# Grouped-query attention on one core: new constants in an instruction planner, one more chain of approximate exponentials, and a bank for the first keys

## The chip, the core and the metric

The kernel runs on one core of a Trainium2 chip. TensorE multiplies matrices into PSUM, ScalarE (ACT) evaluates exponentials, VectorE (DVE) does elementwise work, GpSimd (POOL) and the DMA queues move and cast data. The metric is device time in microseconds (us). The kernel before takes 366.95 us, the median of three runs from 366.82 to 367.03; the profiled execution has a span of 365.6 us.

## What is computed

Batch 8, 8 query heads and 2 key/value heads, sequence 1024, head size 64, all float32 in and out. Four query heads share one key/value head.

```python
scores = scale * np.matmul(q_group, k_group.transpose(0, 1, 3, 2))   # scale = 1/sqrt(64)
attn = np.exp(scores - scores_max)
attn = attn / (np.sum(attn, axis=-1, keepdims=True) + 1e-08)
output = np.matmul(attn, v_group)
```

So there are 64 jobs (8 x 8 heads), each with a 1024 x 1024 matrix of scores, which must be exponentiated, multiplied with the values and divided by its row sums. The inputs are small (0.1 times normal), and the kernel leaves out the subtraction of the maximum.

## The kernel before

**Tiles.** A job's scores come in eight units, one per pair of key blocks. A unit is two matmuls (L537) of 64 x 512, one on each half of the rows of the array, into one of three PSUM slots of 128 x 1024 float32 (sp0, sp1, sp2, two banks each). The scores are transposed: keys lie on partitions, queries along the free dimension. The PV matmuls (L601) take blocks of 128 queries of the exponentials as weights and the values with a column of ones as the moving operand (65 columns), so the row sums come out as column 64. Results gather in two more PSUM banks (op0, op1), seven pieces of 128 queries in a bank. VectorE takes the reciprocal of the sums (L654) and multiplies (L657), and a DMA stores each head.

**Two ways to exponentiate.** Six of a head's eight units go to ScalarE: one activation with Exp (L549), PSUM in, bfloat16 out (tile pt). The other two go to VectorE, which approximates. Its first pass (L560, "dpass") reads the slot and writes 16-bit integers that are the bits of an approximate power of two (tile yt). Then, for two units together (a "chain"), L567 ("zh") and L574 ("two") split mantissa and exponent with bit operations into zt and et, and L583 ("mul") multiplies. The term et is not added by VectorE but by TensorE: a unit of VectorE costs two PV terms per piece instead of one. Only in the last two heads does VectorE add it (L588).

**The order.** The class Plan runs before any instruction is written. It simulates the engines with the constants M_..., in ns, and lists events in the order in which they are to be issued; the kernel then writes them in that order, under a manual schedule. So each engine's queue has a fixed order, and all true times come from semaphores. Some constants are prices (M_ACT an exp, M_ATAIL its tail, M_FIX the fixed part of a VectorE operation, M_DTAIL its tail, M_REC a reciprocal); others are policy. M_RUNWAY says how much work ScalarE may have ahead when a further unit of scores is issued for it, M_BACK how much VectorE may have, M_WAIT how long TensorE holds out for a slot before it turns to PV, M_START and M_SWAP when the slots, ScalarE and VectorE begin, M_WARM until when scores cost double, M_Q1 when the second head's queries are there. MXD is how many of a head's units VectorE may take: `pick_d` chooses the head. When TensorE has nothing else to do early on, it runs dummy matmuls (L429).

**Self-waits.** pt has 32 buffers. When a buffer comes round again it must not be written before its last write is known to be done. Every twelfth exp is given a wait for the exp fifteen before it, so that the framework has that knowledge at hand.

**The start.** The first head's q and k come straight to SBUF, are cast to bfloat16, and turned by TensorE with an identity (L443): four blocks of q into sp1, four of k into sp2. ScalarE copies 384 columns of q out (L453), VectorE the first 128 of k (L454), the rest of q (L455), the rest of k (L456). Then the first scores run, and `swap_k0` builds the copy of k with its halves exchanged (L462, L466).

**Other work.** GpSimd issues DMAs that cast later heads' q and k to bfloat16 in DRAM (L359, L367), and copies the values into the tile va, as bfloat16 with the ones between them (L384), once for each of the 16 key/value heads.

Of the kernel before, what the change touches and what calls it, by code (L numbers as in the profile page):

```python
# [8 lines left out]


M_START = 5850
M_SWAP = 1100
M_Q1 = 3300
M_QSTEP = 2700
M_WARM = 5900
M_FILL = 12000
M_DUMMY = 110
M_SEE = 51
# [2 lines left out]
M_SWITCH = 93  # L21
M_MM = 31.2
M_PVTAIL = 180
M_ACT = 905
M_ATAIL = 135
M_FIX = 76
M_DTAIL = 83
M_DEP = 34
M_D1 = 1.042
M_D2 = 0.521  # L30
M_D4 = 0.261
M_REC = 115
M_GAP = 90
M_RUNWAY = 1500
M_BACK = 3000
M_WAIT = 250
STEP = 10
INF = float("inf")
PB = 7
NPIECE = 8  # L40
GRAIN = 1
MXD = 2
TAIL = 2
STEPS = (("zh", M_D4), ("two", M_D4), ("mul", M_D2), ("add", M_D2))


class Plan:
# [14 lines left out]
    def run(self):  # L62
        nj, ev = self.nj, self.ev
        todo = [list(range(8)) for _ in range(nj)]
        dcount = [0] * nj
        qready = [M_START] + [M_START + M_Q1 + M_QSTEP * j for j in range(nj - 1)]
        slot_free = [M_START, M_START, M_START + M_SWAP - 600]
        aq, dq = [], []
        p_ready = [[INF] * 8 for _ in range(nj)]
        tP = tA = M_START  # L70
        tD = M_START + M_SWAP
        mode = None
# [3 lines left out]
        norms = []  # L76
        out_free = [M_START, M_START]
        pc, done = 0, 0
# [6 lines left out]
        def steps_of(j):  # L85
            return STEPS if j >= nj - TAIL else STEPS[:3]

        def pick_d():
            for j in range(a, min(nj, a + 3)):
                if todo[j] and dcount[j] < MXD and qready[j] <= tP:  # L90
                    return j
            return None

        while pc < last or steps or norms:
# [3 lines left out]
            if tA == t:  # L98
                if aq and aq[0][0] <= t:
                    _, s, j, c = aq.pop(0)  # L100
                    ev.append((t, "act", s, j, c))
                    tA = t + M_ACT
                    slot_free[s] = p_ready[j][c] = tA + M_ATAIL + M_SEE
                else:
                    tA = t + STEP
                continue
            if tD == t:
                end = None
                if dq and dq[0][0] <= t:
                    _, s, j, c = dq.pop(0)  # L110
# [11 lines left out]
                    ev.append((t, "dpass", s, (ch["id"], len(ch["pairs"]) - 1), (j, c)))  # L122
                    end = t + M_FIX + 1024 * M_D1
                    slot_free[s] = end + M_DTAIL + M_SEE
                    dlast = (ch["id"], 0)
# [3 lines left out]
                elif norms and norms[0][0] <= t and norms[0][1] == "rec":  # L129
                    _, _, lo, hi = norms[0]  # L130
                    ev.append((t, "rec", (lo, hi), None, None))
                    end = t + M_REC
                    dlast = lo
                    norms[0] = (end, "norm", lo, hi)
                else:
# [10 lines left out]
                    if best:  # L146
                        at = max(t, dend + M_DEP) if best[0] else t
                        ch = best[2]
                        if ch is None:
                            _, _, lo, hi = norms.pop(0)  # L150
                            ev.append((t, "norm", (lo, hi), None, None))

                            end = at + M_FIX + 64 * min(hi - lo, PB if lo < last else 4) * M_D1
                            out_free[group_of[lo] % 2] = end + M_DTAIL + M_SEE
                            dlast = None
                        else:
                            n = len(ch["pairs"])
                            kind, rate = ch["steps"][ch["at"]]
                            ev.append((t, kind, None, ch["id"], n))
                            end = at + M_FIX + 1024 * n * rate  # L160
                            ch["at"] += 1
                            dlast = (ch["id"], ch["at"])
                            if ch["at"] == len(ch["steps"]):
                                chains.remove(ch)
                                for j, c in ch["pairs"]:
                                    p_ready[j][c] = end + M_DTAIL + M_SEE
                if end:
                    tD, dend = end, end + M_DTAIL
                else:
                    tD = t + STEP  # L170
                continue

            cold = 2 if t < M_WARM else 1
            free = [s for s in range(3) if slot_free[s] <= t]
            runway = tA - t + M_ACT * len(aq)
            slack = runway - cold * M_PAIR - M_PTAIL - (M_SWITCH if mode != "s" else 0)
            can_a = a < nj and len(aq) < 2 and qready[a] <= t and used_p < self.npt
            dj = None
            if not dq and len(chains) < self.nyt and (open_chain or used_c < self.nct):
                back = max(tD - t, 0)  # L180
                for ch in chains:
                    n = len(ch["pairs"])
                    back += sum(M_FIX + 1024 * n * r for _, r in ch["steps"][ch["at"] :])
                if back < M_BACK:
                    dj = pick_d()
            kind = None
            if free:
# [5 lines left out]
                elif can_a:  # L193
                    full = len(free) > 1 or mode == "s"
                    if slack <= M_GAP or (full and runway < M_RUNWAY):
                        kind = "A"
            if kind:
# [4 lines left out]
                j = a if kind == "A" else dj  # L202
                c = todo[j].pop(0)
# [7 lines left out]
                else:  # L211
                    dcount[j] += 1
                    if j < nj - TAIL:
                        self.mms[j] += 1
            elif (
                mode == "s"
                and (dj is not None or (can_a and runway < M_RUNWAY + M_WAIT))
                and any(t < x <= t + M_WAIT for x in slot_free)
            ):
                tP += STEP  # L220
            elif pc < last and (
# [12 lines left out]
                if done == total:  # L234
# [6 lines left out]
                    if pc % NPIECE == 0:  # L241
                        j = pc // NPIECE - 1
# [6 lines left out]
            elif (  # L249
# [12 lines left out]
                c = min(steps, key=lambda c: p_ready[nj - 1][c])  # L262
# [13 lines left out]
            if open_chain and not dq and a >= nj - 2 and pick_d() is None:  # L276
                chains.append(open_chain)
                open_chain = None
# [5 lines left out]
def kernel(  # L284
# [7 lines left out]
    nc = tc.nc  # L292
# [5 lines left out]
    Sync = mybir.DependencyInfo(mybir.DependencyClass.Sync, mybir.DependencyReason.DATA)  # L298
# [14 lines left out]
    NPT = 32  # L313
# [24 lines left out]
    def new_slot(i):  # L338
        sps[i] = banks[f"sp{i}"].tile([128, 2, HS], FP32, name=f"sp{i}")
        return sps[i]  # L340
# [33 lines left out]
    def rows(x, fours=False):  # L374
        how = "(p c two) d -> p c (two d)" if fours else "(c p two) d -> p c (two d)"
        return x.rearrange(how, p=128, two=2)

    def load_v(b, g):
        t = vsp.tile([128, NH, 2 * D], FP32, name="vs")
        vs[(b, g)] = t  # L380
        return nc.sync.dma_start(out=t, in_=rows(v[b, g], b == g == 0))
# [34 lines left out]
    k0, q0 = kt[(0, 0)], qt[0]  # L416
# [20 lines left out]
    nc.scalar.activation(out=b16["k"][:, 1:NH], in_=f32["k"][:, 1:NH], func=AF.Copy)  # L437

    tc.add_manual_dep(load_v(0, 0).ins, ins.ins.name, Sync, reason="loads in time, not sooner")
    turned = {"k": new_slot(2)[:, 0, :], "q": new_slot(1)[:, 0, :]}  # L440

    def turn(x, c):
        nc.tensor.matmul(  # L443
            turned[x][:, c * 128 : (c + 1) * 128],
            lhsT=b16[x][:, c, :], rhs=ident, start=True, stop=True,
        )

    for c in range(NH):
        turn("q", c)
    for c in range(NH):  # L450
        turn("k", c)
    QS = 3 * 128
    nc.scalar.activation(out=q0[:, 0, 0:QS], in_=turned["q"][:, 0:QS], func=AF.Copy)  # L453
    nc.vector.tensor_copy(out=k0[:, 0, 0:128], in_=turned["k"][:, 0:128])  # L454
    nc.vector.tensor_copy(out=q0[:, 0, QS:HS], in_=turned["q"][:, QS:HS])  # L455
    nc.vector.tensor_copy(out=k0[:, 0, 128:HS], in_=turned["k"][:, 128:HS])  # L456

# [13 lines left out]
    for j in range(NJ):  # L471
# [8 lines left out]
        if h % HPG == 0:  # L480
            ev.append((max(pvs[j] - 8000, M_START), "pl", None, (b, g), None))
        if j > 2:
# [17 lines left out]
    exps, stores = [], []  # L500

    def terms(j, par):

        for ci in range(NC):
            c = ci if par == 0 else (ci + NH) % NC
            if (j, c) in where:
                ch, i = where[(j, c)]
                if j < NJ - TAIL:
                    yield ci, et[ch].bitcast(BF16)[:, i, par, :]
# [4 lines left out]
    for when, kind, x, j, c in ev:  # L514
# [31 lines left out]
        elif kind == "act":  # L546
# [1 line left out]
            pt[(j, c)] = p  # L548
            exps.append(nc.scalar.activation(out=p, in_=where_s[(j, c)], func=AF.Exp, scale=scale))  # L549

            if len(exps) % 12 == 0 and len(exps) > 16:
                tc.add_manual_dep(
                    exps[-1].ins, exps[-16].ins.name, Sync, reason="buffers written before"
                )
        elif kind == "dpass":
            ch, i = j
            where[c] = j
            if i == 0:
                yt[ch] = yp.tile([128, 2, 2, HS], U16, name="yt")
            nc.vector.tensor_scalar(  # L560
                out=yt[ch][:, i, :, :], in0=where_s[c],
                scalar1=EXP_A, scalar2=EXP_B, op0=ALU.mult, op1=ALU.add,
            )
        elif kind == "zh":
# [3 lines left out]
                out=zt[j][:, 0:c], in0=yt[j][:, 0:c], scalar1=0x7F, scalar2=0x3F00,  # L568
                op0=ALU.bitwise_and, op1=ALU.bitwise_or,
            )  # L570
        elif kind == "two":
# [3 lines left out]
                out=et[j][:, 0:c], in0=yt[j][:, 0:c], scalar1=0x7F80, scalar2=None,  # L575
# [5 lines left out]
        elif kind == "mul":  # L581
            z = zt[j].bitcast(BF16)[:, 0:c]
            nc.vector.tensor_tensor(  # L583
                out=z, in0=yt[j].bitcast(BF16)[:, 0:c], in1=z, op=ALU.mult
            )
        elif kind == "add":
            z = zt[j].bitcast(BF16)[:, 0:c]
            nc.vector.tensor_tensor(  # L588
                out=z, in0=et[j].bitcast(BF16)[:, 0:c], in1=z, op=ALU.add
# [40 lines left out]
        elif kind == "half":  # L630
# [3 lines left out]
                out=rows(out[b, h])[:, 2 * x : 2 * x + 2],  # L634
                in_=ost[:, r : r + 4, :].rearrange("p (s two) d -> p s (two d)", two=2),
            )
        elif kind in ("rec", "norm"):
# [17 lines left out]
            else:  # L655
                n = min(n, PB if lo < plan.last else 4)
                nc.vector.tensor_tensor(  # L657
                    out=ost[:, r : r + n, :],
# [4 lines left out]
                if lo >= plan.last:  # L663
                    for i in range(4):
                        nc.scalar.activation(  # L665
                            out=ost[:, r + 4 + i, :], in_=o2[:, 1, i, 0:D],
                            func=AF.Copy, scale=rec[:, 4 + i : 5 + i],
                        )
        elif kind == "store":
# [3 lines left out]
                out=rows(out[b, h], j == 0),  # L673
                in_=ost[:, r : r + NPIECE, :].rearrange("p (s two) d -> p s (two d)", two=2),
# [32 lines left out]
```

## Time and profile before

| engine | busy us, share of the span | what it does |
|---|---|---|
| ScalarE | 356.4, 97% | 384 exps on line L549, 352.8 us |
| VectorE | 353.4, 97% | 128 first passes 156.0, 64 products 81.6, 72 normalizations 44.3, L567 44.2, L574 42.6, reciprocals 14.2 |
| TensorE, matmul | 345.7, 95% | 1024 score matmuls 172.0 and 5024 PV matmuls |
| TensorE, weight load | 219.5, 60% | |
| GpSimd | 49.8, 14% | 78 DMA issues 38.2, 16 copies of values 11.2 |

TensorE's clock was granted in full (0.999). The DMA engines moved 44.81 MB, 123 GB/s on average. In the list of waits, TensorE's scores waited 6.5 us in all for ScalarE to release a slot (28 times, 0.4 us at most) and 3.6 us for VectorE (12 times); ScalarE's exps waited 1.6 us for scores, VectorE's first passes 0.8.

How to read it: busy time is the union of the spans of an engine's instructions. One exp's span is 1.135 us on average, while 384 of them fit into 352.8 us: a span includes the tail [...], and the next instruction starts within it. A wait that is shorter than the tail does not show as idle time. The spacing from start to start, in the timeline, is what an instruction takes from its engine.

The last exp starts at 358.9 us, the last PV matmuls run from 360.11 to 361.03, and the last normalization on VectorE starts at 361.31; after it come the last stores.

### The profile page before, as it was taken

The page shows a single profiled execution, that of the slowest core. Times are in us where ns is not written, and L with a number is a line of the kernel's source. Part 1 is how long each engine was busy: PE and PEld are TensorE (multiplying, and loading weights), DVE is VectorE, ACT ScalarE, POOL GpSimd, SP SyncE. Part 2 cuts the span into 40 slices and gives each one's busy share as a digit, 9 for nine tenths or more (in the row PEclk, how much of TensorE's full clock was granted, in tenths as well). Part 3 has the DMA queues.
Part 4 walks back from the last instruction along what each step waited for, and adds up shares of the span by engine and source line. Part 5 has one row for each costly group of instructions (what it writes and reads, how often), then busy time and mean ns, then how long its engine had stood idle before and what let it go on. Part 6 is the DMA issues. An engine that isn't in the chain of part 4 may idle for free. (4 is left out here: it accounts for less than half of the span.)

```text
span 365.6 us, 13820 instructions
## 1 busy us (share of the span) xinstructions
PE 345.7 (95%) x6161; PEld 219.5 (60%) x6161; DVE 353.4 (97%) x476; ACT 356.4 (97%) x392; POOL 49.8 (14%) x100
## 2 busy tenths in 40 slices
PE   7899999999999999999999999999999999999994
PEld 3465665666656666566566565666656666556663
DVE  3999999999999999999999999999999999999995
ACT  5999999999999999999999999999999999999995
POOL 4002031121201112021111112012021011111000
PEclk9999999999999999999999999999999999999999
DMA  7446585566664975678764868667496667577213
GB/s 172 88 88 128 111 168 97 134 149 124 121 120 105 148 148 112 148 114 128 131 112 104 168 102 152 127 137 119 85 158 122 158 102 147 118 130 107 74 34 113
DMA packets 89307, 44.81 MB, mean 123 GB/s; under 512 B 45504, under 2 KB 87616, under 8 KB 88000
## 3 DMA queue, kind: packets, MB, share of 16 engines
q1 hardware_dynamic: 86336, 33.31, 40.5%
q0 software_dynamic: 2496, 10.23, 21.9%
q8 instruction: 48, 0.79, 0.9%
q10 hardware_dynamic: 416, 0.39, 0.3%
q14 instruction: 11, 0.09, 0.1%
HBM read 25.17 MB, written 27.00 MB: 143 GB/s over the span
## 5 line engine op out<-in xcount | busy, mean ns | idle before, releaser
L549 ACT ACTIVATE pt<-sp 128x1024 bf16<-128x1024 f32 x384 | 352.8, 1135 | 1.6 <-PE sp L537 1.6
L601 PE MATMUL ops<-va,pt 128*128 128x65 bf16 x3024 | 186.1, 194 | 0.0
L537 PE MATMUL sp<-qt,kt 64*128 64x512 bf16 x1024 | 172.0, 382 | 13.9 <-ACT pt L549 6.5
L601 PEld LDWEIGHTS <-pt 128*128 128x128 bf16 x3024 | 134.9, 97 | 48.3 <-issue 48.3
L560 DVE TENSOR_SCALAR yt<-sp 128x1024 uint16<-128x1024 f32 x128 | 156.0, 1219 | 1.8 <-PE sp L537 0.8
L601 PE MATMUL ops<-va,zt 128*128 128x65 bf16 x1008 | 120.6, 194 | 0.0
L601 PE MATMUL ops<-va,et 128*128 128x65 bf16 x992 | 118.8, 194 | 0.0
L601 PEld LDWEIGHTS <-et 128*128 128x128 bf16 x992 | 80.1, 98 | 17.6 <-issue 16.2
L601 PEld LDWEIGHTS <-zt 128*128 128x128 bf16 x1008 | 81.4, 97 | 14.5 <-issue 14.2
L583 DVE TENSOR_TENSOR zt<-yt,zt 128x2048 bf16<-128x2048 bf16 x64 | 81.6, 1275 | 0.0
L537 PEld LDWEIGHTS <-kt 64*128 64x128 bf16 x1024 | 46.1, 93 | 55.3 <-issue 34.0
L359 POOL DMA_DIRECT2D qd<-in_q_dram x63 | 30.8, 489 | 228.4 <-PE sp L537 223.0
L657 DVE TENSOR_TENSOR ost<-ops,rec 128x448 f32<-128x448 f32 x72 | 44.3, 615 | 0.0
L567 DVE TENSOR_SCALAR zt<-yt 128x2048 uint16<-128x2048 uint16 x64 | 44.2, 691 | 0.0
L574 DVE TENSOR_SCALAR et<-yt 128x2048 uint16<-128x2048 uint16 x64 | 42.6, 666 | 0.0
L367 POOL DMA_DIRECT2D kd<-in_k_dram x15 | 7.4, 493 | 55.2 <-PE sp L537 50.4
L654 DVE RECIPROCAL rec<-ops 128x7 f32<-128x7 f32 x72 | 14.2, 198 | 0.5 <-PE ops L601 0.2
L384 POOL CAST va<-vs 128x512 bf16<-128x512 f32 x16 | 11.2, 700 | 1.2 <-DMA vs<-in_v_dram 1.1
L429 PE MATMUL ops<-warm 128*128 128x128 bf16 (+1 forms) x33 | 5.5, 320 | 1.2 <-DVE warm L351 1.2
L429 PEld LDWEIGHTS <-warm 128*128 128x128 bf16 x33 | 2.4, 108 | 4.1 <-issue 2.9
L434 DVE CAST k<-k 128x128 bf16<-128x128 f32 x1 | 0.2, 226 | 2.5 <-DMA k<-in_k_dram 2.5
L665 ACT ACTIVATE ost<-sp,rec 128x64 f32<-128x64 f32 x4 | 0.9, 315 | 1.8 <-PE sp L622 1.8
(30 smaller groups left out, 16.5 us busy)
## 6 DMA issues: line engine op xcount, KB each, us to landing
out_dram<-ost SPq DMA_DIRECT2D x63, 256.0 KB, 2.9
qd<-in_q_dram POOLq DMA_DIRECT2D x63, 128.0 KB, 3.5
vs<-in_v_dram SPq DMA_DIRECT2D x16, 256.0 KB, 4.0
kd<-in_k_dram POOLq DMA_DIRECT2D x15, 128.0 KB, 3.5
kt<-kt SPq DMA_DIRECT2D x30, 64.0 KB, 3.5
qt<-qd SPq DMA_TRANSPOSE x63, 4.0
q<-in_q_dram ACTq DMA_DIRECT2D x1, 256.0 KB, 3.3
kt<-kd SPq DMA_TRANSPOSE x15, 3.4
```

What stands on the lines that cost most here:

```text
L359: return nc.gpsimd.dma_start(out=t.rearrange("(a x) d -> a (x d)", x=4), in_=q[b, h].rearrange("(a x) d -> a (x d)", x=8),)
L384: return nc.gpsimd.tensor_copy(out=va[:, b * G + g, :, :, 0:D], in_=vs.pop((b, g)).rearrange("p c (two d) -> p c two d", two=2),)
L429: nc.tensor.matmul(ops[1][:, 0:cols], lhsT=warm[:, 0:128], rhs=warm[:, 0:cols], start=True, stop=True)
L537: now = nc.tensor.matmul(sps[x][:, half, :], lhsT=t[lo : lo + D, c // NH, ci % NH * 128 : (ci % NH + 1) * 128], rhs=qt[j][lo : lo + D, 0, ...
L549: exps.append(nc.scalar.activation(out=p, in_=where_s[(j, c)], func=AF.Exp, scale=scale))
L560: nc.vector.tensor_scalar(out=yt[ch][:, i, :, :], in0=where_s[c], scalar1=EXP_A, scalar2=EXP_B, op0=ALU.mult, op1=ALU.add,)
L567: nc.vector.tensor_scalar(out=zt[j][:, 0:c], in0=yt[j][:, 0:c], scalar1=0x7F, scalar2=0x3F00, op0=ALU.bitwise_and, op1=ALU.bitwise_or,)
L574: ins = nc.vector.tensor_scalar(out=et[j][:, 0:c], in0=yt[j][:, 0:c], scalar1=0x7F80, scalar2=None, op0=ALU.bitwise_and,)
L583: nc.vector.tensor_tensor(out=z, in0=yt[j].bitcast(BF16)[:, 0:c], in1=z, op=ALU.mult)
L601: nc.tensor.matmul(ops[plan.group_of[x] % 2][:, lo : lo + D + 1], lhsT=p[:, qs * 128 : (qs + 1) * 128], rhs=va[:, b * G + h // HPG, ci % N ...
L654: nc.vector.reciprocal(out=to, in_=sums)
L657: nc.vector.tensor_tensor(out=ost[:, r : r + n, :], in0=o[:, :, 0:D], in1=rec[:, 0:n].unsqueeze(2).to_broadcast([128, n, D]), op=ALU.mult,)
```

## The change

It has four parts.

1. **Constants of the plan.** The prices of an exp, of VectorE's fixed part and of the tails are set anew, and so are the policy constants. This is meant to bring the plan closer to the measured times, so that the order that it finds fits the chip.
2. **A third unit for VectorE in two heads.** `pick_d` allows three instead of two in heads whose number is 1 modulo 32 (heads 1 and 33). Two units make one chain. They leave ScalarE.
3. **Rarer self-waits.** Every 26th exp waits for the one five before it, instead of every twelfth for the one fifteen before it.
4. **The start.** The first block of k is turned into sp0, a bank of its own, and ScalarE takes 320 instead of 384 columns of the first q.

```diff
-M_START = 5850
-M_SWAP = 1100
-M_Q1 = 3300
+M_START = 5800
+M_SWAP = 1500
+M_Q1 = 3400
-M_WARM = 5900
+M_WARM = 6400
-M_ACT = 905
-M_ATAIL = 135
-M_FIX = 76
-M_DTAIL = 83
+M_ACT = 917
+M_ATAIL = 107
+M_FIX = 66
+M_DTAIL = 80
-M_REC = 115
+M_REC = 90 
-M_RUNWAY = 1500
-M_BACK = 3000
-M_WAIT = 250
+M_RUNWAY = 2200
+M_BACK = 2500
+M_WAIT = 300
...
+MORE = 32
...
-                if todo[j] and dcount[j] < MXD and qready[j] <= tP:
+                if todo[j] and dcount[j] < MXD + (j % MORE == 1) and qready[j] <= tP:
...
-    turned = {"k": new_slot(2)[:, 0, :], "q": new_slot(1)[:, 0, :]}
+    turned = {"k": new_slot(2)[:, 0, :], "q": new_slot(1)[:, 0, :], "k0": new_slot(0)[:, 0, :]}
...
-            turned[x][:, c * 128 : (c + 1) * 128],
+            turned["k0" if x == "k" and c == 0 else x][:, c * 128 : (c + 1) * 128],
...
-    QS = 3 * 128
+    QS = 320
...
-    nc.vector.tensor_copy(out=k0[:, 0, 0:128], in_=turned["k"][:, 0:128])
+    nc.vector.tensor_copy(out=k0[:, 0, 0:128], in_=turned["k0"][:, 0:128])
...
-            if len(exps) % 12 == 0 and len(exps) > 16:
+            if len(exps) % (NPT - 6) == 0:
                 tc.add_manual_dep(
-                    exps[-1].ins, exps[-16].ins.name, Sync, reason="buffers written before"
+                    exps[-1].ins, exps[-6].ins.name, Sync, reason="buffers written before"
                 )
```

## The prediction

> **What bounds the kernel now.** I read the page first, for the load of each engine:
>
> ```profile
> PE 345.7 (95%) x6161; PEld 219.5 (60%) x6161; DVE 353.4 (97%) x476; ACT 356.4 (97%) x392; POOL 49.8 (14%) x100
> L549 ACT ACTIVATE pt<-sp 128x1024 bf16<-128x1024 f32 x384 | 352.8, 1135 | 1.6 <-PE sp L537 1.6
> L560 DVE TENSOR_SCALAR yt<-sp 128x1024 uint16<-128x1024 f32 x128 | 156.0, 1219 | 1.8 <-PE sp L537 0.8
> L583 DVE TENSOR_TENSOR zt<-yt,zt 128x2048 bf16<-128x2048 bf16 x64 | 81.6, 1275 | 0.0
> ```
>
> Three engines are full, so the question is which one really has room. [...] So I went to the timeline of ScalarE, where exps that follow each other without a visible gap are merged:
>
> ```profile
> 6.84 27.74 ACT L549 ACTIVATE pt<-sp 128x1024 bf16<-128x1024 f32 x30 [1.11 <-PE sp L537]
> ...
> 109.93 5.74 ACT L549 ACTIVATE pt<-sp 128x1024 bf16<-128x1024 f32 x6
> 115.84 2.91 ACT L549 ACTIVATE pt<-sp 128x1024 bf16<-128x1024 f32 x3 [0.16 <-PE sp L537]
> ```
>
> Thirty exps in 27.74 us are (27.74 - 1.14)/29 = 0.917 us apart; from the first start (6.84) to the last (358.9, the answer on line L549) the mean is 352.05/383 = 0.919. The closest spacing in the trace is 0.904 (thirteen in a row from 66.88 to 78.63 us). So ScalarE needs 383 x 0.904 = 346.2 us and loses about 5.8 in waits too short to be listed as idle.
>
> The same for VectorE. Its timeline gives the spacing of each operation, start to start:
>
> ```profile
> 111.50 2.01 DVE L583 TENSOR_TENSOR zt<-yt,zt 128x2048 bf16<-128x2048 bf16 x1
> 113.43 1.21 DVE L560 TENSOR_SCALAR yt<-sp 128x1024 uint16<-128x1024 f32 x1
> ...
> 115.24 1.21 DVE L560 TENSOR_SCALAR yt<-sp 128x1024 uint16<-128x1024 f32 x1
> 116.37 0.61 DVE L657 TENSOR_TENSOR ost<-ops,rec 128x448 f32<-128x448 f32 x1
> 116.90 0.68 DVE L574 TENSOR_SCALAR et<-yt 128x2048 uint16<-128x2048 uint16 x1
> 117.50 0.19 DVE L654 RECIPROCAL rec<-ops 128x7 f32<-128x7 f32 x1
> 117.62 1.17 DVE L583 TENSOR_TENSOR zt<-yt,zt 128x2048 bf16<-128x2048 bf16 x1
> 118.71 1.21 DVE L560 TENSOR_SCALAR yt<-sp 128x1024 uint16<-128x1024 f32 x1
> 119.84 0.61 DVE L657 TENSOR_TENSOR ost<-ops,rec 128x448 f32<-128x448 f32 x1
> 120.37 0.68 DVE L567 TENSOR_SCALAR zt<-yt 128x2048 uint16<-128x2048 uint16 x1
> 120.97 1.21 DVE L560 TENSOR_SCALAR yt<-sp 128x1024 uint16<-128x1024 f32 x1
> ```
>
> A first pass (L560) takes 1.13, L567 and L574 take 0.60 each, a product (L583) 1.09 to 1.13, a normalization (L657) 0.53 and its reciprocal (L654) 0.115. With the counts of the page: 128 x 1.13 + 64 x (0.60 + 0.60 + 1.11) + 2 x 1.09 (L588) + 73 x 0.645 = 342 us of pure work. VectorE runs from 7.80 (first pass) to 361.31 (last normalization), 353.5 us. The missing 11.5 us have two parts. The product of 111.50 took 2.01 instead of 1.2, because GpSimd was copying values at that moment:
>
> ```profile
> 111.80 0.63 POOL L384 CAST va<-vs 128x512 bf16<-128x512 f32 x1
> ```
>
> That slot came free late, and the exp of 115.84 above started 0.46 us late. Products average 1.275 against 1.17 to 1.22 undisturbed, so about 64 x 0.075 = 4.8 us, and L567 (0.691 against 0.64 to 0.69) adds some 0.7: **5.5 us of collisions**. The other **6 us are waits**: 0.57 between the first two passes, 0.75 before the last reciprocals, and some 4.7 spread over the middle. TensorE waited 6.5 us for ScalarE's slots and 3.6 for VectorE's, so it is close behind. No engine has 2% to give; VectorE has 6 us of waits, ScalarE 5.8.
>
> [...] the first key copy (L454), which needs one key block, starts at 5.67, after the fourth block was turned (5.63), [...] the trace shows 0.904, which I use.
>
> **The change part by part.** From the instruction lists of both programs as built: 382 exps for 384, 130 first passes for 128, 65 each of L567, L574 and L583 for 64, 5040 PV matmuls for 5024.
>
> *ScalarE:* two exps fewer, 2 x 0.904 = -1.8 us. This counts only where ScalarE sets the end.
>
> *VectorE:* heads 1 and 33 get a third pair, together one more chain: 2 x 1.13 + 0.60 + 0.60 + 1.11 = **+4.6 us**. Nothing is taken from it.
>
> *TensorE:* 16 more matmuls at 0.031 = +0.5. With the wider runway scores come in longer stretches: 253 stretches for 278. A change from scores to PV and back costs about 0.19: 0.32 instead of 0.22 from a score pair to the next matmul (351.89 to 352.21), 0.13 instead of 0.03 the other way. So 25 x 0.19 = -4.8, net -4.3. TensorE gets room; since VectorE and ScalarE are full, it shows only as fewer waits for scores.
>
> *Self-waits:* 16 exps wait for an earlier exp where 31 did. The answer on L549 has each as a separate instruction of 17 ns on ScalarE's queue; the exps around them are 0.904 apart, so the queue is ahead and I cost it at nothing. What it waits for is five exps back instead of fifteen, about 4.5 us old, and long done; no other work is queued behind a wait that is already fulfilled.
>
> *Start:* the first keys have a bank of their own, so their copy need not wait for the fourth key block: 5.35 instead of 5.67 (the first turn starts at 5.00 and takes 0.31). The other gate is q: ScalarE copies 320 columns instead of 384 (0.49 becomes 0.44), then VectorE 192 instead of 128 (0.28 becomes 0.35), and VectorE's copy still waits for ScalarE's, [...]. It ends near 6.09 instead of 6.16. Gain: **0.1 us** (the full 0.3 of the key copy if q were no gate; I take 0.1). The second VectorE score is one place later in TensorE's order, behind one more score (0.22): it gives back about that 0.1 on VectorE.
>
> *The constants* (exp 917, fixed part of VectorE 66 and so on) cost nothing themselves; they only choose the order. Planned with 917 while 0.904 is possible, ScalarE can catch up after a late score, by 13 ns an exp. With 66 for 76, VectorE is planned at its true speed and can't catch up after a collision.
>
> **Sum.** VectorE is the path: 342 + 4.6 + 5.5 (collisions, 16 copies as before) = 352 us of occupied time inside a stretch that was 353.5. The end moves by -0.1 + 0.1 + 4.6 less the waits that vanish. At most the 4.7 of the middle can vanish; the 1.3 at both ends follow from the data. That bound is 366.95 + 4.6 - 4.7 = 366.85, with nothing won. I expect 3.5 of the 4.7 to vanish, since ScalarE has 1.8 and TensorE 4.3 us more room, while some passes remain just in time: +4.6 - 3.5 = +1.1, **368.0 us**, chance 0.50; with 2.5 to 4.7 vanishing it covers 366.9 to 369.0. What TensorE and ScalarE give is thus mostly spent in filling VectorE.
>
> **Rivals.** *ScalarE still sets the end* and the pair lies in waits of VectorE that nobody needed: then -1.8 - 0.1 = 365.05, and up to 1 us less if the 13 ns of catching up also take stalls away. For it: the last exp (358.9 + 1.14) is what the last PV waits for in the chain of waits, and ScalarE's stalls are 5.8 us. Against it: VectorE would have to lose all middle waits and 2 us of collisions. The collisions are a matter of which operation the 16 copies fall on: they cost 0.1 to 0.83 each here, so a spread of about 1.1 on 5.5. I put this case at 365.3; chance 0.28.
> *VectorE's waits stay*, because its passes remain just in time or because collisions fall on more products: only 2 of 4.7 vanish, 366.95 + 4.6 - 2.0 = 369.5; chance 0.22. If none vanished it would be 371.5, which the room won on TensorE speaks against.
>
> **From these to the numbers.** Slower by over 0.2% (over 367.7): all of the last case and a little over half of the forecast's, 0.50. Within 0.2% (366.2 to 367.7): the rest of the forecast's, 0.22. Faster: 0.28. Range 365.2 to 369.6: it leaves out the lower half of the faster case's spread and the far end of the slow one, and takes in the spread of collisions.
>
> **What would show it.** VectorE's timeline with fewer gaps before L560, and from first pass to last normalization about 354.6 us; exps spaced 0.92 to 0.93 on average, wider than before, as ScalarE now waits for slots that VectorE holds; waits of TensorE for yt up, for pt down; first exp near 6.75; 253 score stretches with no price on the end. It would be wrong if the mean of L583 fell to about 1.2 (collisions gone), or if the exps closed up to 0.91: then the end falls with ScalarE.

## The result: slower by 0.56%, and the profile after

The changed kernel takes 368.86 us (median of 6 runs, 368.5 to 369.98) against 367.01 before (6 runs on the same chip): a ratio of 1.0056, 95% interval 1.0042 to 1.0071. The prediction said 368.0, slower. The direction and the engine were right; one term of its sum was mis-sized, another changed by chance, and a stretch in which TensorE has almost no work was not foreseen.

The page after, with the loads of the engines and the shares of the chain that ended last, then the groups that answer to those of before (lines have moved by one: L549 is L550, L560 is L561, L567 is L568, L574 is L575, L583 is L584). This profile was taken in a run of 369.62 us, one of the two slowest of the six:

```profile
PE 349.1 (95%) x6177; PEld 221.6 (60%) x6177; DVE 355.2 (97%) x481; ACT 356.6 (97%) x390; POOL 51.1 (14%) x100
...
DVE 72%; ACT 18%; PE 8%; issue 1%; ACTq 0%
...
L550 ACT ACTIVATE pt<-sp 128x1024 bf16<-128x1024 f32 x382 | 353.0, 1063 | 3.9 <-PE sp L538 3.3
...
L561 DVE TENSOR_SCALAR yt<-sp 128x1024 uint16<-128x1024 f32 x130 | 158.1, 1216 | 2.0 <-PE sp L538 2.0
...
L584 DVE TENSOR_TENSOR zt<-yt,zt 128x2048 bf16<-128x2048 bf16 x65 | 78.8, 1212 | 0.0
...
L568 DVE TENSOR_SCALAR zt<-yt 128x2048 uint16<-128x2048 uint16 x65 | 46.8, 720 | 0.2
L575 DVE TENSOR_SCALAR et<-yt 128x2048 uint16<-128x2048 uint16 x65 | 44.9, 691 | 0.0
```

ScalarE does two exps fewer and is as busy as before: its exps stand 0.9315 us apart (first start 6.56, last 361.47, 381 steps) instead of 0.919. It waits more (3.9 us idle before exps, where it was 1.6), and the chain runs through VectorE for 72% of the span. In the list of waits TensorE's scores now wait longer for VectorE's slots than for ScalarE's, the reverse of before. First the kernel before, then the changed one (total, times, longest):

```profile
PE sp L537 <- ACT pt L549: 6.5, 28, 0.4
PE sp L537 <- DVE yt L560: 3.6, 12, 0.5
```

```profile
PE sp L538 <- DVE yt L561: 5.0, 18, 1.0
...
PE sp L538 <- ACT pt L550: 3.6, 10, 0.5
ACT pt L550 <- PE sp L538: 3.3, 6, 0.9
DVE yt L561 <- PE sp L538: 2.0, 4, 0.8
```

**VectorE's account.** From each trace I took VectorE's stretch from its first pass to its last normalization, and split it: collisions (what an operation's span exceeds its group's median by, where over 30 ns), waits (gaps beyond the usual 75 ns of overlap, where over 25 ns), and the rest, work. All in us. "Half clock" is how long TensorE's clock was at half between its first rise and the end of the matmuls; the last column is the device time of that same profiled run.

| kernel | stretch | work | collisions | waits | half clock | run |
|---|---|---|---|---|---|---|
| before | 353.5 | 341.7 | 5.6 | 6.2 | 0 | 367.42 |
| changed | 356.1 | 346.5 | 4.2 | 5.4 | 6.83 | 369.62 |
| changed, a later profile | 355.6 | 346.5 | 4.2 | 4.9 | 3.41 | 368.70 |
| third units in heads 33 and 49 | 353.7 | 346.2 | 3.9 | 3.6 | 0 | 367.57 |
| before, values by DMA | 353.8 | 342.1 | 0.0 | 11.7 | 3.41 | 367.66 |
| changed, values by DMA | 352.6 | 346.5 | 0.5 | 5.6 | 6.83 | 366.86 |
| changed, dummies planned in | 352.4 | 346.4 | 2.1 | 3.9 | 0 | 365.91 |
| changed, dummies put in after planning | 356.2 | 346.4 | 5.3 | 4.5 | 0 | 369.81 |
| both: dummies planned in, values by DMA | 350.5 | 346.2 | 0.4 | 4.0 | 0 | 364.96 |

The run exceeds VectorE's stretch by 13.1 to 14.5 us in all nine, so the stretch tells the time to within 0.7 us or so. From before to changed it grows by 2.6: work +4.8, collisions -1.4, waits -0.8. In the later profile of the changed kernel, whose run is closer to the median, it grows by 2.1: the same work and collisions, waits -1.3.

**A stretch that I had not foreseen.** The table of stretches shows TensorE after the first head's PV (columns: stretch, its length, busy time and instructions of TensorE's matmuls and weight loads, VectorE, ScalarE, GpSimd, granted clock, DMA share, GB/s):

```profile
20.00:22.00 2.00, 0.94 (x6) 0.19 (x4) 2.00 (x5) 2.00 (x3) 0.26 (x1) 1.00 0.64 98
22.00:24.00 2.00, 1.22 (x6) 0.30 (x6) 2.00 (x3) 2.00 (x4) 0.00 (x0) 0.74 0.56 164
24.00:26.00 2.00, 1.87 (x14) 0.87 (x14) 2.00 (x4) 2.00 (x4) 0.54 (x1) 0.50 0.29 66
26.00:28.00 2.00, 2.00 (x31) 1.47 (x29) 2.00 (x3) 1.27 (x2) 0.02 (x1) 0.50 0.51 74
28.00:30.00 2.00, 2.00 (x21) 0.81 (x19) 1.20 (x2) 1.43 (x2) 0.00 (x0) 0.55 0.00 0
```

From 20 to 24 us TensorE has six matmuls in each 2 us, scores alone. The kernel before has 42 and 38 in the same time:

```profile
20.00:22.00 2.00, 2.00 (x42) 1.25 (x39) 2.00 (x5) 2.00 (x3) 0.00 (x0) 1.00 0.67 185
22.00:24.00 2.00, 2.00 (x38) 1.23 (x34) 2.00 (x3) 2.00 (x3) 0.00 (x0) 1.00 0.30 68
```

Head 1's third unit is the first half of a chain whose second half comes from head 2, so head 1's PV must wait for it. By the plan this goes on until head 33's third unit closes it: 32 chains in a row straddle two heads, where none does in the kernel before. In the thin stretch the clock falls to half (0.50 from 22.97 to 29.79), and PV matmuls and scores arrive late at both other engines. ScalarE's timeline and VectorE's:

```profile
27.56 1.02 ACT L550 ACTIVATE pt<-sp 128x1024 bf16<-128x1024 f32 x1 [0.73 <-PE sp L538]
29.15 31.68 ACT L550 ACTIVATE pt<-sp 128x1024 bf16<-128x1024 f32 x34 [0.57 <-PE sp L538]
```

```profile
27.57 1.22 DVE L584 TENSOR_TENSOR zt<-yt,zt 128x2048 bf16<-128x2048 bf16 x1
29.58 1.23 DVE L561 TENSOR_SCALAR yt<-sp 128x1024 uint16<-128x1024 f32 x1 [0.80 <-PE sp L538]
31.34 0.21 DVE L655 RECIPROCAL rec<-ops 128x7 f32<-128x7 f32 x1 [0.54 <-PE ops L602]
```

With the hidden part of the gaps that is 0.87 + 0.61 = 1.5 us of VectorE's 5.4 us of waits. The half clock lasts 6.83 us here and 3.41 in two other profiles of this kernel; the first rise to full clock lies 5.90 us into the span here and 6.66 in the kernel before. In the 3.41 us before the fall TensorE was lightly loaded, not idle: its matmuls were busy for 1.99 of them.

### The profile page after: what moved, and what is told of

Its sections match the earlier page's. It is cut to its first block, busy times and chain, and to the rows that moved or that the text cites. A ratio compares the mean times of both kernels' runs of the same rounds, so it can differ in the third digit from the quotient of the medians.

```text
span 367.8 us, 13833 instructions
## 1 busy us (share of the span) xinstructions
PE 349.1 (95%) x6177; PEld 221.6 (60%) x6177; DVE 355.2 (97%) x481; ACT 356.6 (97%) x390; POOL 51.1 (14%) x100
## 4 chain that ended last, share of the span: by engine, by line
DVE 72%; ACT 18%; PE 8%; issue 1%; ACTq 0%
DVE yt L561 30%; ACT pt L550 18%; DVE zt L584 15%; DVE zt L568 8%; DVE ost L658 8%; DVE et L575 8%; PE sp L538 3%; PE ops L602 3%; DVE rec L655 2%; PE ops L430 1%; PE sp L623 1%; ACT ost L666 0%; ACT qt L454 0%; PE sp L444 0%; DVE qt L456 0%
## 5 line engine op out<-in xcount | busy, mean ns | idle before, releaser
L550 ACT ACTIVATE pt<-sp 128x1024 bf16<-128x1024 f32 x382 | 353.0, 1063 | 3.9 <-PE sp L538 3.3
L538 PE MATMUL sp<-qt,kt 64*128 64x512 bf16 x1024 | 175.0, 385 | 12.8 <-DVE yt L561 5.0
L602 PE MATMUL ops<-va,pt 128*128 128x65 bf16 x3008 | 181.3, 194 | 0.0
L602 PEld LDWEIGHTS <-pt 128*128 128x128 bf16 x3008 | 144.5, 98 | 33.5 <-issue 33.5
L561 DVE TENSOR_SCALAR yt<-sp 128x1024 uint16<-128x1024 f32 x130 | 158.1, 1216 | 2.0 <-PE sp L538 2.0
L602 PE MATMUL ops<-va,zt 128*128 128x65 bf16 x1024 | 137.3, 195 | 0.2 <-DVE zt L584 0.2
L602 PE MATMUL ops<-va,et 128*128 128x65 bf16 x1008 | 135.8, 195 | 0.0
L602 PEld LDWEIGHTS <-et 128*128 128x128 bf16 x1008 | 88.7, 98 | 23.5 <-issue 23.5
L602 PEld LDWEIGHTS <-zt 128*128 128x128 bf16 x1024 | 90.2, 98 | 14.6 <-issue 13.9
L584 DVE TENSOR_TENSOR zt<-yt,zt 128x2048 bf16<-128x2048 bf16 x65 | 78.8, 1212 | 0.0
L360 POOL DMA_DIRECT2D qd<-in_q_dram x63 | 33.4, 530 | 227.5 <-PE sp L538 213.8
L568 DVE TENSOR_SCALAR zt<-yt 128x2048 uint16<-128x2048 uint16 x65 | 46.8, 720 | 0.2
L575 DVE TENSOR_SCALAR et<-yt 128x2048 uint16<-128x2048 uint16 x65 | 44.9, 691 | 0.0
```

Source lines behind the costliest of these rows:

```text
L360: return nc.gpsimd.dma_start(out=t.rearrange("(a x) d -> a (x d)", x=4), in_=q[b, h].rearrange("(a x) d -> a (x d)", x=8),)
L538: now = nc.tensor.matmul(sps[x][:, half, :], lhsT=t[lo : lo + D, c // NH, ci % NH * 128 : (ci % NH + 1) * 128], rhs=qt[j][lo : lo + D, 0, ...
L561: nc.vector.tensor_scalar(out=yt[ch][:, i, :, :], in0=where_s[c], scalar1=EXP_A, scalar2=EXP_B, op0=ALU.mult, op1=ALU.add,)
L568: nc.vector.tensor_scalar(out=zt[j][:, 0:c], in0=yt[j][:, 0:c], scalar1=0x7F, scalar2=0x3F00, op0=ALU.bitwise_and, op1=ALU.bitwise_or,)
L575: ins = nc.vector.tensor_scalar(out=et[j][:, 0:c], in0=yt[j][:, 0:c], scalar1=0x7F80, scalar2=None, op0=ALU.bitwise_and,)
L584: nc.vector.tensor_tensor(out=z, in0=yt[j].bitcast(BF16)[:, 0:c], in1=z, op=ALU.mult)
```

## The experiments

Theory A: VectorE's load sets the end of the changed kernel, and what hits VectorE adds to the time. Theory B: head 1's third unit starves TensorE, its clock falls, and that alone makes it slower.

**The third units elsewhere.**

```diff
-                if todo[j] and dcount[j] < MXD + (j % MORE == 1) and qready[j] <= tP:
+                if todo[j] and dcount[j] < MXD + (j in (33, 49)) and qready[j] <= tP:
```

> The changed kernel with its third units in heads 33 and 49 instead of 1 and 33. Same counts on every engine (382 exps, 130 first passes, 5040 PV matmuls). In the changed kernel TensorE has hardly any work from 20 to 24 us (6 matmuls in 2 us), its clock falls to half from 22.97 to 29.79 us, and two exps start 0.96 and 0.69 us late. Theory A (VectorE's load alone makes it slower): 368.5 to 369.0, as the changed kernel. Theory B (the third unit of head 1 holds back that head's PV, TensorE idles, and its clock falls): no half clock around 25 us and 1.0 to 1.9 us less, 366.9 to 367.8.

367.25 us, ratio to before 0.9998 (0.999 to 1.0006): the same as before, and 1.6 us below the changed kernel with the same counts. TensorE's stretch is filled and its clock full:

```profile
20.00:22.00 2.00, 1.70 (x34) 1.08 (x31) 2.00 (x5) 2.00 (x3) 0.00 (x0) 1.00 0.69 110
22.00:24.00 2.00, 1.89 (x29) 0.98 (x28) 2.00 (x3) 2.00 (x3) 0.00 (x0) 1.00 0.32 69
```

By itself this speaks for B. In the account: waits 3.6 instead of 5.4, collisions about the same. So 4.5 us more work than before were paid by 2.6 us of waits and 1.7 of collisions.

**No third units.** The condition is `MXD + 0`; all else as changed.

> The changed kernel without third units: 384 exps, 128 first passes, all else as in the changed kernel. Theory A (VectorE's 4.6 us set the end): 2 to 4 us faster than the changed kernel, at or below the 367.0 of before. Theory B (the half clock after head 1): 1 to 2 us faster than the changed kernel, near 367. Theory C (the new prices give a worse order of their own, since the exp is priced at 917 with nothing moved off ScalarE, which stretches the plan): slower than the changed kernel, 370 or more, with stretches of TensorE without PV work.

371.18 us, ratio 1.0113 (1.0099 to 1.0127). Theory C (the new prices give a worse order of their own) had the number: with the new constants and nothing moved off ScalarE, the planner finds an order that is worse than before by 4 us. Prices and policy constants changed together, so it is not shown that the price of 917 does it. VectorE waits for PV results near the end, as its list of waits shows:

```profile
DVE rec L655 <- PE ops L602: 5.2, 2, 3.7
```

So the new constants and the third units belong together, and constants do cost something of their own, through the order that they make. What third units do alone, under the old constants, was not measured.

**Start and self-waits alone.** The kernel before with only these parts of the diff.

> The kernel before with the first keys in their own bank, 320 columns of the first q on ScalarE, and the rarer self-waits; prices, policy and third units as before. All theories: 0 to 0.2 us faster than before, 366.8 to 367.0; first exp about 0.1 to 0.3 us earlier, spacing of the exps unchanged. A rival: the self-waits do cost something, 31 to 16 of them: 0.3 us or more faster.

367.06 us, ratio 0.9994 (0.9986 to 1.0002): nothing that can be measured, as expected. In its profile the exps stand 0.9188 us apart, before 0.9192.

**The third units in heads 9 and 41,** `MXD + (j in (9, 41))`.

> The changed kernel with its third units in heads 9 and 41. As in head 1, the third unit of head 9 closes its chain only with a unit of the next head, and the list of TensorE's work has a long stretch of scores without PV near 63 us; head 41's doesn't matter as much. Theory B (a stretch of some 5 us with only scores lets TensorE's clock fall): half clock for some 7 us from about 66 us on, and 368 to 369, as the changed kernel. Rival (only the start, where the clock has just come up, is sensitive): no fall, 367.0 to 367.5, as with heads 33 and 49.

367.93 us, ratio 1.0014 (1.0003 to 1.0025). Its 22 runs fall in two groups by mean granted clock: 8 runs at 0.997 or 0.998 took 366.6 to 367.15 us, 14 runs at 0.992 or 0.993 took 367.8 to 368.85. The profiled run is of the first group and shows no fall, so where the clock fell in the others was not seen. It does have a stretch like that of the changed kernel, with 6 and 11 matmuls in the 2 us from 64 and from 66 us, and 32 chains over two heads, and yet at a full clock it is no slower than the kernel before. In this kernel the lower clock goes with some 1.4 us, and it came in 14 of 22 runs of the same program.

**Values without copies on GpSimd.** In the kernel before and in the changed one, values are cast by two DMAs per head straight into va:

```diff
...
+        if (b, g) != (0, 0):
+            for i in range(2):
+                ins = nc.gpsimd.dma_start(
+                    out=va[:, b * G + g, :, i, 0:D], in_=rows(v[b, g])[:, :, i * D : (i + 1) * D]
+                )
...
+            return ins
...
-            place_v(*j)
+            if j == (0, 0):
+                place_v(*j)
```

Like the other casts, each also gets the dependency on the last score.

> The kernel before, with the values of all key/value heads but the first cast by two DMAs each straight into va, instead of a load, and a copy by GpSimd: 15 of the 16 copies that collide with VectorE are gone. Collision theory (5.5 us of VectorE's time here, and what it loses can't be won back since ScalarE is planned without slack): 2 to 5 us faster, 362 to 365, products at 1.21 us on average. Rival (the lost time lies in waits anyway, or the DMAs' issue on GpSimd blocks VectorE as much as the copies did): 366.5 to 367.5.

> The same in the changed kernel. If VectorE sets its end outside the stretch of half clock, the 4.2 us of collisions come back nearly in full: 364 to 365.5. If the half clock alone makes it slower and VectorE has room: 368 to 369, as the changed kernel.

The kernel before gains almost nothing: 366.58, ratio 0.999 (0.9981 to 0.9999); the 2 to 5 us of the collision theory did not come. The changed kernel gains 3.85 us: 365.01, ratio 0.9936 (0.9921 to 0.9951). Counting only runs with a mean clock of 0.996 or more, the gains are much the same, 0.6 us (medians 367.1 and 366.6) and 3.9 us (368.9 and 364.9). These are the lines of one collision in the changed kernel, on VectorE and then on GpSimd; L575 takes 1.36 us where its mean is 0.69:

```profile
53.59 1.36 DVE L575 TENSOR_SCALAR et<-yt 128x2048 uint16<-128x2048 uint16 x1
54.87 1.21 DVE L561 TENSOR_SCALAR yt<-sp 128x1024 uint16<-128x1024 f32 x1
```

```profile
53.77 0.63 POOL L385 CAST va<-vs 128x512 bf16<-128x512 f32 x1
```

The account tells the two kernels apart. Before, 5.6 us of collisions go and 5.5 us of waits come (6.2 to 11.7), on the same stretch. Some 1.1 us of these waits belongs to the run that was profiled: its clock was at half from 15.17 to 18.59 us (the line below shows part of it), and behind that stand four waits, from 17.7 to 28.9 us, that the kernel before doesn't have. The five runs of this kernel at a mean clock of 0.992 took 367.57 to 367.72, where the median of those at 0.996 or more is 366.57. The other 4.4 us or so of waits took the place of collisions: VectorE was not this kernel's bound, and its first passes now just wait for scores.

```profile
16.00:18.00 2.00, 2.00 (x25) 1.07 (x23) 1.71 (x4) 1.50 (x2) 0.00 (x0) 0.50 0.32 74
```

The groups of that kernel without copies show it: products fell from 1275 to 1203 ns, and the idle time before first passes rose from 1.8 to 4.0.

```profile
L569 DVE TENSOR_SCALAR yt<-sp 128x1024 uint16<-128x1024 f32 x128 | 156.2, 1220 | 4.0 <-PE sp L546 2.1
L592 DVE TENSOR_TENSOR zt<-yt,zt 128x2048 bf16<-128x2048 bf16 x64 | 77.0, 1203 | 0.0
```

In the changed kernel, where both profiles have 6.83 us of half clock, 3.7 us of collisions go, waits stay (5.4 and 5.6), and the stretch shrinks by 3.5. That is Theory A: VectorE has become the bound, and a collision costs nearly its full length.

> Third units in heads 33 and 49, and the values cast by DMA. Its steps of delay in the trace of that kernel with copies (3.9 us from start to end against the planned order) each stand at a copy that hit VectorE. Collision theory: 3 to 4 us faster than with copies, 363.0 to 364.3, faster than both kernels. Rival (VectorE's load, not collisions): 366.5 to 367.3.

366.05, ratio 0.9964 (0.995 to 0.9977): faster than both kernels, but 1.2 us below the same kernel with copies instead of the 3 to 4 expected. In its trace 1.6 us of collisions remain: each stands at a DMA that GpSimd issues for the values, and these slow L568 and L575 by 0.03 to 0.25 us at a time.

**The changed kernel again,** for its runs by clock, and for one more profile.

> The changed kernel once more, to sort its runs by the granted clock. Theory B (the stretch without PV after head 0 lets TensorE's clock fall, by chance or not, and the fall is what makes it slower): runs with a mean clock of 0.99 to 0.995 at 368.5 to 370, and any run at 0.997 or more at 367.0 to 367.5, as with third units in heads 33 and 49. Rival (the order as such, with copies that hit VectorE and a PV backlog, makes it slower, and the fall adds little): runs with a full clock also at 368 or more.

> One more profile of the changed kernel, for a trace in which TensorE's clock may stay full after head 0. If the order alone costs the time: the same span within 0.5 us, and the time that is not lost at 25 us is lost at copies later on.

368.89 us, ratio 1.005 (1.0036 to 1.0063); the one further run took 368.91. The rival is right: runs at 0.998, 1.0 and 1.0 took 368.64 to 368.90, those at 0.993 and 0.994 took 368.93 and 368.70. So the fall of the clock is not what makes this kernel slower than before. A longer one seems to add to it: in the first six runs the two at 0.991, one of them with the 6.83 us of half clock of the page above, took 369.62 and 369.98, the others 368.5 to 368.9. Both new profiles had the fall (3.41 us of it), and their two late arrivals at VectorE came to 0.9 us instead of 1.5; a trace of this kernel with a full clock was not seen.

**Dummies that keep TensorE busy,** planned in:

```diff
+            elif t < 26000 and pc == NPIECE and done == 0:
+                ev.append((tP, "keep", None, None, None))
+                tP += M_DUMMY
+                mode = "v"
...
+        elif kind == "keep":
+            nc.tensor.matmul(
+                ops[1][:, 256:512], lhsT=warm[:, 0:128], rhs=warm[:, 0:256], start=True, stop=True
+            )
```

> The changed kernel with 23 more dummy matmuls of 256 columns, some 0.11 us each, in the stretch after head 0 where TensorE has scores and no PV (into columns of op1 that hold nothing yet). Theory B: the clock stays full there in all runs, and 1 to 1.9 us less than the changed kernel, 367.0 to 367.8. Rival (the order as such): clock full, but still 368 or more.

> The dummy matmuls and the values cast by DMA together. The changed kernel with values cast by DMA took 364.7 to 365.0 in runs with a full clock and 365.6 to 366.9 in the others. Theory B: all runs at 364.5 to 365.2, 2 us below the kernel before. Rival (the dummies cost as much in delayed scores as the clock gains): 365.5 to 366.5.

365.81, ratio 0.9967 (0.9954 to 0.9979), 3.1 us below the changed kernel, more than either theory said; and 365.11, ratio 0.9948 (0.9935 to 0.996), with values by DMA. But the dummies also move the plan behind them: in the account, waits fell by 1.5 and collisions by 2.1. Which of these is due to the clock?

**The same dummies without a new plan,** three after each score pair in that stretch:

```diff
+            if 19600 < when < 25000:
+                for _ in range(3):
+                    nc.tensor.matmul(
+                        ops[1][:, 256:512], lhsT=warm[:, 0:128], rhs=warm[:, 0:256],
+                        start=True, stop=True,
+                    )
```

> The changed kernel with three dummy matmuls of 256 columns after each of the nine score pairs in the stretch without PV, put in after planning: the order of all other instructions is that of the changed kernel, where the earlier dummies also moved the plan behind them. If the fall of the clock and the late exps at 25 us make the changed kernel slower: 366.9 to 367.6. If its order makes it slower (where the 16 copies of values fall on VectorE: 4.2 us of them there, 2.1 in the kernel whose plan knew of the dummies): 368.3 to 368.9, as those runs of the changed kernel that had a full clock, with the collisions of the changed kernel in the trace.

369.68 us, ratio 1.0068 (1.0052 to 1.0084): with a full clock (0.998 to 1.0 in all six runs) it is not faster, but slower than either theory said. Where the waits of 29.58 and 31.34 were, a collision has come, because the copy now falls on L574 (L568 of the changed kernel) at 30.69. The clock in that time, then VectorE, then GpSimd:

```profile
22.00:24.00 2.00, 1.91 (x15) 0.79 (x12) 2.00 (x3) 1.68 (x3) 0.00 (x0) 1.00 0.43 126
24.00:26.00 2.00, 2.00 (x15) 0.83 (x13) 1.96 (x3) 2.00 (x3) 0.00 (x0) 1.00 0.29 66
```

```profile
30.69 1.56 DVE L574 TENSOR_SCALAR zt<-yt 128x2048 uint16<-128x2048 uint16 x1
```

```profile
31.07 0.62 POOL L385 CAST va<-vs 128x512 bf16<-128x512 f32 x1
```

It costs 0.88 us. In the changed kernel this copy, at 32.20, hit nothing. Another collision is 0.2 longer, and the dummies themselves delay one score by 0.68. Together that is 1.8 us, a little more than the 1.5 that the full clock gave. The dummies cost something themselves, so this kernel is not a clean test of the clock alone; the runs of the changed kernel at a full clock, 368.64 to 368.90, are. With both, B falls as the cause of the 1.85 us. The fall is one of the things that hit a VectorE without slack, and here its place is taken by another.

## Why the prediction came out right, and where its steps were off

- **VectorE as the path:** right, and shown by the pair of kernels without copies. In before, most of a collision was absorbed in waits; in the changed kernel it is not. The end is an exception: the chain's last stretch, from 345.10 us on, is mostly ScalarE (17 exps) and then TensorE.
- **+4.6 us of work:** measured +4.8.
- **3.5 us of waits vanish:** this is the mis-sized term. Only 0.8 vanished (6.2 to 5.4), or 1.3 in the later profile. With the third units in heads 33 and 49, 2.6 did. Of the shortfall, 1.5 us (0.9 in the later profile) is the two late arrivals at 29 to 31 us; the rest was not traced.
- **Collisions as before, 5.5:** measured 5.6 before and 4.2 after, about the spread of 1.1 that was named. The account thus gives +4.8 - 0.8 - 1.4 = +2.6; the first pass starts 0.29 us earlier (7.51 for 7.80), which leaves +2.3. The two profiled runs differ by 2.2. That 368.0 came so close to 368.86 is therefore in part luck: with collisions of 5.5 the same kernel would stand near 370, an estimate from this account.
- **The sign of being wrong, a mean of about 1.2 for L583:** it came (1275 to 1212 ns) and did not mean what it was taken for. Collisions did not go; they moved from the products to L567 and L574, whose means rose from 691 to 720 and from 666 to 691 ns (after: L568 and L575 above). Six of the changed kernel's seven collisions over 30 ns stand there. Before:

```profile
L567 DVE TENSOR_SCALAR zt<-yt 128x2048 uint16<-128x2048 uint16 x64 | 44.2, 691 | 0.0
L574 DVE TENSOR_SCALAR et<-yt 128x2048 uint16<-128x2048 uint16 x64 | 42.6, 666 | 0.0
```

- **ScalarE's spacing of 0.92 to 0.93, waits for yt up and for pt down:** as predicted, or just above (0.9315; 5.0 and 3.6). VectorE's stretch was to be about 354.6 and was 356.1.
- **TensorE's room shows only as fewer waits:** wrong. I counted PV matmuls and changes over the whole span, not where they stand. The room came as an almost empty stretch behind head 0, and the waits for scores rose, from 1.6 to 3.3 us on ScalarE and from 0.8 to 2.0 on VectorE.
- **Start 0.1 us:** the first exp starts 0.28 earlier, but the first q also landed 0.23 earlier in that run (its cast starts at 3.86 for 4.09), so 0.05 is left. The key copy starts at 5.36 (5.35 was worked out), before the fourth key block is turned (5.63), and q is the gate: ScalarE's copy of it ends at 5.69, VectorE's runs from 5.72 to 6.08. **Self-waits at nothing:** the experiment agrees.
- **The rival in which ScalarE sets the end** is refuted: with two exps fewer the kernel is slower, and ScalarE waits more than before. The rival in which VectorE's waits stay had the better term (0.8 to 1.3 vanished, of the 4.7 that could), offset by fewer collisions.

What stays open: how the changed kernel loses its time in runs with a full clock. The kernel with dummies after planning suggests a collision near 30 us, but that kernel is another one. Nor does VectorE's extra work settle it alone: kernels with the same counts took 365.81 (but for its dummies, planned in), 366.6 to 367.15 (heads 9 and 41, full clock), 367.25 (heads 33 and 49) and 368.86. Which feature of an order makes this difference was not isolated; it is not the chains over two heads as such, since the first two of these have 32 of them as well.

## What to carry to other kernels

Before work is moved onto an engine, ask what its waits are for. Here the waits of an engine that was not the bound absorbed collisions almost for free; once its slack was filled, collisions cost nearly their full length (5.6 us of them were worth 0.6 us in one order and 3.7 were worth 3.85 in the other). And look at a planned order stage by stage: two orders with equal counts differed by 1.6 us, and the table of stretches showed at once that one of them left TensorE almost empty for 4 us, which no count shows. Where a small addition re-plans everything behind it, test it once with the old order kept, or its effect can't be told from luck.

## What the runs showed that I had not expected

TensorE's clock fell to half, for 3.41 or 6.83 us, in some runs of a kernel and not in others, and what a fall cost differed by kernel: nothing that shows in the changed one (3.41 us of it), some 1.4 us with heads 9 and 41. What decides whether it falls was not shown. A light load alone does not: in the changed kernel TensorE's matmuls were busy for 1.99 of the 3.41 us before the fall, but in the kernel before they were busy for only 1.91 of the 3.41 us from 11.97, and its clock stayed full, as it did in the thin stretch of the profile with heads 9 and 41. First the changed kernel, then the kernel before:

```profile
19.56:22.97 3.41, 1.99 (x18) 0.65 (x16) 3.41 (x7) 3.41 (x5) 0.49 (x1) 1.00 0.68 140
```

```profile
11.97:15.38 3.41, 1.91 (x14) 0.58 (x12) 3.41 (x5) 3.41 (x5) 0.49 (x1) 1.00 0.47 85
```

The DMAs that GpSimd issues for the values, with third units in heads 33 and 49, slow VectorE's 0.69 us operations by 0.03 to 0.25 us, where its copies of 0.63 us cost up to 0.9. Its issues for q and k show no such cost: in the changed kernel 20 of L568 and L575 overlap one and no copy, and take 0.64 to 0.69 us, where those that overlap neither take 0.64 to 0.70. And the best order found here, with third units in heads 1 and 33 and values cast by DMA, is 2.1 us faster than the kernel before (365.01 and 367.14); with the planned dummies as well it is 2.0 faster (365.11 and 367.1).
